# Inverses in two diagonal blocks with small products, an end in halves, squares added on DVE

## The chip, the cores and the metric

The kernel runs on one core of a Trainium2 chip. The metric is the device time of one execution in microseconds (us). PE is TensorE, DVE VectorE, ACT ScalarE, POOL GpSimd; SP issues most of the DMAs.

## The reference

One decoder block for 512 tokens of width 2048, in fp32. Two branches work on the normed input: RWKV-7 time mixing (16 heads of 64, a recurrence over the tokens) and a chunked spatial gate. They are mixed by sigmoid gates and added to the input; a SwiGLU layer of 5,632 hidden columns follows, and a last RMSNorm. Cut to what matters here:

```python
p = _rmsnorm(x, g) @ w_in                    # r, k, v, low-rank inputs, SGU input, gates
def step(S, inp):                            # RWKV-7, per head, S is 64 x 64
    sa = jnp.einsum('bhij,bhj->bhi', S, a_t)
    S = S * w_t[:, :, None, :] + sa[..., None] * b_t[:, :, None, :] + v_t[..., None] * k_t[:, :, None, :]
    y_t = jnp.einsum('bhij,bhj->bhi', S, r_t)
h = x + gates * branches
h = h + (silu(n(h) @ w_gate) * (n(h) @ w_up)) @ w_down
out = _rmsnorm(h, norm_final_g)
```

## The kernel before

Activations lie transposed, channels on partitions, 512 tokens along a row. Each fp32 product is made of three fp32r matmuls: ACT casts a weight tile to `w_hi` (`hi_of`, L105), DVE subtracts to get `w_lo` (`lo_of`, L108), and `mm3` (L125 to L127) multiplies hi by hi, hi by lo and lo by hi. A scheduler that simulates the engines decides the order of instructions on each engine; `tc.high_priority()` moves work forward in it.

The work in order of time: *the start* (0 to about 50 us), where the input arrives, is scaled and split (`a`, L161) and its squares are summed (L213, L214); 12 blocks of r, k and v; from 416 us 16 *gate blocks* of 96 matmuls of 128x512 (`ps_big`), whose results (`gt`, L524) go to DRAM; the spatial gate, the merge, the SwiGLU layer, and the down-projection from 2280 us on.

The recurrence is done in 8 chunks of 64 tokens. For every head and chunk (128 units) a unit triangular 64x64 matrix, loaded as `Ld`, one unit per partition, is inverted by substitution on DVE: 63 steps of one multiply (L406) and one reduce (L408) for each of two halves of the rows, into `X`. `X` goes to DRAM (`d_x`), and the chain of 8 chunk steps loads each step's part as `cTI` (L428) and the operands as `crec` (L418). The chain's fp32 matmuls (L472, L481, L490, L508, L511) stand between block matmuls.

The down-projection has 44 tiles of hidden rows (k). Its *main loop* runs over two halves of the output (q = 0, 1) and 40 of the tiles. *The end* takes the other four tiles, for 256 tokens at a time (H0, then H1): `down_sq` loads and splits weights of two output tiles, multiplies, adds to `hA` (L733), squares on ACT and sums on POOL (L856); then come the sum over partitions by a ones matmul (L171), a reciprocal of two columns, a diagonal matrix `dg` and a matmul that spreads it (L179), and `scale_out` (L887 and L889), which stores pairs of tiles.

Of the kernel before, what the change touches and what calls it, by code (L numbers as in the profile page):

```python
# [9 lines left out]
F32 = mybir.dt.float32  # L10
# [41 lines left out]
def body(ctx: ExitStack, tc: tile.TileContext, xT, par, cst, w_l0, w_in, lup, gup, sguw, sgub, lng, lnb,  # L52
# [22 lines left out]
    d_x = dram.tile([2, 64, 64, 64], F32, name="d_x")  # L75
# [121 lines left out]
    for n in START:  # L197
        pl = None
        for k in range(k0, k0 + n):
            nc.sync.dma_start(out=xt[:, k, :], in_=xT[k])  # L200
            if pl is None:
                pl = chunk(w_l0, k0, n, 2 * LORA)
            nT.append(scaled_split(xt[:, k, :], P("g1", k), ap, "a"))
        pg = chunk(w_in[0], k0, n, 256)
        if k0 <= 4 < k0 + n:
            nc.sync.dma_start(out=cst_t, in_=cst)
            nc.sync.dma_start(out=ident, in_=cst[:, 0:128])
        for k in range(k0, k0 + n):
            if k == 0:
                act.activation(out=acc, in_=xt[:, 0, :], func=AF.Square)  # L210
                continue
            sq = st.tile([128, 512], F32, name="sq", bufs=3)
            act.activation(out=sq, in_=xt[:, k, :], func=AF.Square)  # L213
            pool.tensor_tensor(out=acc, in0=acc, in1=sq, op=ALU.add)  # L214
        k0 += n
        if k0 == KT:
            rms(acc, 4, rs_c, st.tile([128, 512], F32, name="sq", bufs=3), rs)
        block_mm(lo_ps, pl, KT, nT, (LORA, LORA))
        block_mm(g_ps, pg, KT, nT, (128, 128))
# [171 lines left out]
    with ExitStack() as cs:  # L391
        gtp = cs.enter_context(tc.tile_pool(name="gtp", bufs=1, side="right"))
        with tc.tile_pool(name="sub", bufs=1, side="right") as sb:
            Ld = sb.tile([128, 64, 64], F32, name="Ld")
            nc.sync.dma_start(out=Ld.rearrange("u s t -> u (s t)"), in_=d_l.rearrange("h u s t -> (h u) (s t)"))
            X = sb.tile([128, 64, 64], F32, name="X")
            pool.memset(X, 0.0)
            pool.memset(X.rearrange("u s t -> u (s t)")[:, 0:4096:65], 1.0)
            for t in range(1, 64):
                for s0, s1 in ((0, min(t, 32)), (32, t)):  # L400
                    n, k = s1 - s0, t - s0
                    if n <= 0:
                        continue
                    tmp = sb.tile([128, 2048], F32, name="tmp", bufs=1)
                    tv_ = tmp[:, 0:n * k].rearrange("u (s k) -> u s k", k=k)
# [10 lines left out]
        def load(c, hf):  # L416
            rec = cp.tile([128, 2304], F32, name="crec", bufs=4)
            nc.sync.dma_start(out=rec, in_=d_c[hf, c])  # L418
            ZY = rec[:, 0:1024].rearrange("r (f h t) -> r f h t", f=4, h=2)
            SLV = rec[:, 1024:2048].rearrange("r (f h t) -> r f h t", f=4, h=2)  # L420
            RB = rec[:, 2048:2304].rearrange("r (f t) -> r f t", f=4)
            SV = cp.tile([128, 4, 2, 64], F32, name="cSV", bufs=4)
            for h in range(2):
                ot = slice(64 - 64 * h, 128 - 64 * h)
                pool.tensor_copy(out=SV[ot, :, h, :], in_=SLV[ot, :, h, 64:128])
            TI = cp.tile([128, 4, 64], F32, name="cTI", bufs=4)
            for h in range(2):
# [417 lines left out]
    at2 = [x for k in range(MAIN // 2, NHID // 2) for x in hidden(k, fin, "z")]  # L845
    acc = fin.tile([128, 512], F32, name="acc3")
    H0, H1 = T1, T2
    rbs = rs[:, 0:256]

    def sum_sq(j, sl):  # L850
        if j == 0:
            act.activation(out=acc[:, sl], in_=hT[j][:, sl], func=AF.Square)
        else:
            sq = fin.tile([128, 512], F32, name="sq2", bufs=2)
            act.activation(out=sq[:, sl], in_=hT[j][:, sl], func=AF.Square)
            pool.tensor_tensor(out=acc[:, sl], in0=acc[:, sl], in1=sq[:, sl], op=ALU.add)  # L856

    def down_sq(b, ts):
        n = NHID - MAIN
        with tc.high_priority():  # L860
            wh, wl = down_w(w_dn[b // 4, MAIN:NHID, :, 256 * (b % 4):256 * (b % 4) + 256].rearrange("k r c -> r k c"),
                            n, 256)
        res = []
        for i in range(2):
            j = 2 * b + i
            ps = bank()[:, 0:256]
            for k in range(n):
                c = slice(128 * i, 128 * i + 128)
                mm3(ps, wh[:, k, c], wl[:, k, c], at2[k][0][:, ts], at2[k][1][:, ts], k == 0, k == n - 1)
            add(hT[j][:, ts], ps, hT[j][:, ts])  # L870
        for j in (2 * b, 2 * b + 1):
            if b == 7:
                sq = fin.tile([128, 512], F32, name="sq2", bufs=2)
                with tc.high_priority():
                    act.activation(out=sq[:, ts], in_=hT[j][:, ts], func=AF.Square)
                res.append(sq[:, ts])
# [4 lines left out]
    def scale_out(p, ts, rb, on_pool):

        for k in (2 * p, 2 * p + 1):
            o = hT[k][:, ts]
            if on_pool(k):
                act.mul(o, o, P("g3", k))
                pool.tensor_tensor(out=o, in0=o, in1=rbs, op=ALU.mult)  # L887
            else:
                dve.scalar_tensor_tensor(out=o, in0=o, scalar=P("g3", k), in1=rb, op0=ALU.mult, op1=ALU.mult)  # L889
        ks = slice(2 * p, 2 * p + 2)  # L890
        nc.sync.dma_start(out=out[ks, :, ts].rearrange("k p t -> p k t"), in_=hA[:, ks, ts])

    for b in range(8):
        sqs = down_sq(b, H0)
    col = cols.pop()
    dg = fin.tile([128, 512], F32, name="dg", bufs=2)
    rb = rms([acc[:, H0]] + sqs, 2, col, dg)
    act.copy(out=rbs, in_=rb)
    for b in range(8):
        sqs = down_sq(b, H1)  # L900
        scale_out(b, H0, rbs, lambda k: k % 2 == 1)
    col = cols.pop()
    dg = fin.tile([128, 512], F32, name="dg", bufs=2)
    rb = rms([acc[:, H1]] + sqs, 2, col, dg)
    act.copy(out=rbs, in_=rb)
    for p in range(8):
        scale_out(p, H1, rb, lambda k: k // 2 in (1, 4, 6))
# [81 lines left out]
```

## Time and profile before

| | us |
|---|---|
| median of three runs | 2787.81 (2785.8 to 2789.99) |
| the profiled execution, own time | 2787.32 |
| its span | 2785.6 |
| PE busy in it | 2717.0 |
| DVE busy | 1839.5 |
| ACT busy | 1009.0 |
| POOL busy | 123.6 |

The span runs from the first instruction to the last; 1.7 us of the profiled execution lie outside of it. PE is nearly always at work, so an average over the span tells little: what counts are the short stretches in which PE waits or runs at a lower granted clock.

### The profile page before, as it was taken

How to read it: one execution, taken by the hardware profiler on the slowest of the kernel's cores; microseconds unless marked ns; L12 is line 12 of the kernel's file. 1: busy time of each engine (PE TensorE's matmuls, PEld its weight loads, DVE VectorE, ACT ScalarE, POOL GpSimd, SP SyncE). 2: the span in 40 equal slices, each digit the busy share in tenths (PEclk: the TensorE clock that was granted, in tenths of full speed). 3: DMA queues.
4: the chain of work that ended last, by engine and by line, in shares of the span. 5: the costliest groups of instructions: out<-in, count | busy, mean ns of one | idle time of the engine just before them, and what ended most of it. 6: DMA issues, size and time to landing. Idle time of an engine off the chain costs nothing.

```text
span 2785.6 us, 41408 instructions
## 1 busy us (share of the span) xinstructions
PE 2717.0 (98%) x17128; PEld 2410.0 (87%) x17128; DVE 1839.5 (66%) x2120; ACT 1009.0 (36%) x1239; POOL 123.6 (4%) x149
## 2 busy tenths in 40 slices
PE   8999999989999999999999999999999999999997
PEld 6888888777799878878799999999999998888887
DVE  6566668999554664435588888888888863333336
ACT  5445432211243332223344444443444432222224
POOL 3000000000111200000000000000000000000005
PEclk9999999999999999999999999999999999999998
DMA  5456664333764524434433433333433354444443
GB/s 169 116 149 154 172 162 151 106 108 105 244 206 145 185 96 140 141 114 148 148 118 118 122 114 122 113 121 113 123 115 118 121 186 159 144 147 148 139 156 122
DMA packets 200046, 388.46 MB, mean 139 GB/s; under 512 B 55857, under 2 KB 101041, under 8 KB 197553
## 3 DMA queue, kind: packets, MB, share of 16 engines
q1 hardware_dynamic: 199712, 385.74, 44.9%
q8 instruction: 134, 2.20, 0.3%
q14 instruction: 56, 0.45, 0.0%
q10 hardware_dynamic: 144, 0.07, 0.0%
HBM read 330.18 MB, written 55.57 MB: 138 GB/s over the span
## 4 chain that ended last, share of the span: by engine, by line
PE 84%; DVE 9%; issue 4%; DMA 1%; POOL 1%; ACT 0%; SPq 0%; POOLq 0%; DVEq 0%; ACTq 0%
PE ps_big L127 10%; PE ps_big L125 10%; PE ps_big L126 10%; PE rkps L125 6%; PE rkps L126 6%; PE rkps L127 6%; PE gB L725 4%; PE gB L727 4%; PE gB L726 4%; PE gA L725 3%; PE gA L727 3%; PE gA L726 3%; DVE tmp L406 3%; DVE w_lo L108 2%; DVE X L408 2%
## 5 line engine op out<-in xcount | busy, mean ns | idle before, releaser
L127 PE MATMUL ps_big<-a,w_lo 128*128 128x512 f32 (+1 forms) x1344 | 532.1, 396 | 28.4 <-DVE w_lo L108 28.4
L125 PE MATMUL ps_big<-a,w_hi 128*128 128x512 f32 (+1 forms) x1344 | 529.5, 394 | 9.0 <-ACT w_hi L105 9.0
L108 DVE TENSOR_TENSOR w_lo<-wq,w_hi 128x1024 fp32r<-128x1024 f32 x272 | 332.5, 1223 | 302.8 <-ACT w_hi L105 300.3
L126 PE MATMUL ps_big<-a,w_hi 128*128 128x512 f32 (+1 forms) x1344 | 528.7, 394 | 0.1
L105 ACT CAST w_hi<-wq 128x1024 fp32r<-128x1024 f32 x272 | 285.7, 1051 | 597.6 <-PE rkps L126 305.2
L108 DVE TENSOR_TENSOR w_lo<-w_raw,w_hi 128x1024 fp32r<-128x1024 f32 (+2 forms) x220 | 272.9, 1242 | 238.1 <-ACT w_hi L105 237.2
L105 ACT CAST w_hi<-w_raw 128x1024 fp32r<-128x1024 f32 (+2 forms) x220 | 225.6, 1030 | 502.2 <-PE ps_big L126 444.6
L127 PEld LDWEIGHTS ps_big<-a,w_lo 128*128 128x128 f32 (+1 forms) x1344 | 253.9, 189 | 94.9 <-DVE w_lo L108 40.4
L125 PEld LDWEIGHTS ps_big<-a,w_hi 128*128 128x128 f32 (+1 forms) x1344 | 254.0, 189 | 63.3 <-ACT w_hi L105 9.7
L126 PEld LDWEIGHTS ps_big<-a,w_hi 128*128 128x128 f32 (+1 forms) x1344 | 254.1, 189 | 55.4 <-DVE a L161 0.6
L125 PE MATMUL rkps<-xh,w_hi 128*128 128x512 f32 x640 | 248.8, 391 | 2.0 <-ACT xh L105 2.0
L126 PE MATMUL rkps<-xl,w_hi 128*128 128x512 f32 x640 | 249.5, 390 | 0.0
L127 PE MATMUL rkps<-xh,w_lo 128*128 128x512 f32 x640 | 249.4, 390 | 0.0
L725 PE MATMUL gB<-xsh,w_hi 128*128 128x256 f32 x704 | 200.2, 284 | 2.4 <-DVE u L733 2.0
L105 ACT CAST w_hi<-wt 128x1024 fp32r<-128x1024 f32 x132 | 138.4, 1049 | 175.6 <-PE gB L726 68.0
L726 PE MATMUL gB<-xsl,w_hi 128*128 128x256 f32 x704 | 200.0, 284 | 0.0
L727 PE MATMUL gB<-xsh,w_lo 128*128 128x256 f32 x704 | 199.9, 284 | 0.0
L108 DVE TENSOR_TENSOR w_lo<-wt,w_hi 128x1024 fp32r<-128x1024 f32 x132 | 161.4, 1223 | 32.6 <-ACT w_hi L105 32.6
L406 DVE TENSOR_TENSOR tmp<-X,Ld 128x1 f32<-128x1 f32 (+46 forms) x94 | 141.5, 1505 | 6.6 <-DMA Ld<-d_l 4.4
L125 PEld LDWEIGHTS rkps<-xh,w_hi 128*128 128x128 f32 x640 | 120.4, 188 | 27.4 <-ACT xh L105 2.2
L126 PEld LDWEIGHTS rkps<-xl,w_hi 128*128 128x128 f32 x640 | 120.5, 188 | 25.1
L127 PEld LDWEIGHTS rkps<-xh,w_lo 128*128 128x128 f32 x640 | 120.4, 188 | 25.0
(598 smaller groups left out, 5722.1 us busy)
## 6 DMA issues: line engine op xcount, KB each, us to landing
wq<-w_gu SPq DMA_DIRECT2D x176, 512.0 KB, 3.6
w_raw<-w_in SPq DMA_DIRECT2D x145, 512.0 KB, 4.0
wq<-w_dn SPq DMA_DIRECT2D x96, 512.0 KB, 4.1
wq<-d_hid SPq DMA_DIRECT2D x42, 512.0 KB, 3.6
crec<-d_c SPq DMA_DIRECT2D x16, 1152.0 KB, 7.4
w_raw<-w_out SPq DMA_DIRECT2D x32, 512.0 KB, 3.9
d_hid<-sl SPq DMA_DIRECT2D x44, 256.0 KB, 2.0
w_raw<-w_ps SPq DMA_DIRECT2D x16, 512.0 KB, 4.2
```

The costliest lines, as they stand in the source:

```text
L105: act.copy(out=dst, in_=src)
L108: (eng or dve).tensor_tensor(out=dst, in0=src, in1=hi.bitcast(F32), op=ALU.subtract)
L125: pe.matmul(out, wh, xh, start=start, stop=False)
L126: pe.matmul(out, wh, xl, start=False, stop=False)
L127: pe.matmul(out, wl, xh, start=False, stop=stop)
L406: dve.tensor_tensor(out=tv_, in0=X[:, s0:s1, s0:t], in1=Ld[:, s0:t, t].unsqueeze(1).to_broadcast([128, n, k]), op=ALU.mult)
L408: dve.tensor_reduce(out=X[:, s0:s1, t], in_=tv_, axis=AX.X, op=ALU.add)
L725: pe.matmul(bank, wh, xh, start=first and k == 0, stop=False, skip_group_check=True)
L726: pe.matmul(bank, wh, xl, start=False, stop=False, skip_group_check=True)
L727: pe.matmul(bank, wl, xh, start=False, stop=k == 7, skip_group_check=True)
```

## The change

It has three parts. *Start*: the 15 additions of squares go from POOL to DVE. *Inverses*: the substitution is done in the two 32x32 diagonal blocks alone, both in one instruction, 31 steps; two ACT copies turn the blocks of `Ld` into `LD`, so that each multiply reads a row. The off-diagonal block is the product of the first inverse, a block of `Ld` (`NB`) and the second inverse, made by PE as 2x128 matmuls of 32x32 in four groups of 32 partitions, with the inverses stored to DRAM (`d_dt`, `d_dx`) and loaded in another layout (`R1`, `R2`). The result (`XO`) is stored too (`d_xo`), and each `cTI` is put together from three loads in place of one, and a zeroed quarter. *End*: the weights of the last four tiles are loaded and split once, in the second half of the main loop, and kept (`wzp`); squares are added on DVE; the norm sums with 256-column ones matmuls and takes a reciprocal of 256 columns; the first 256 tokens (TA) are scaled on DVE alone; the last stores are of four tiles each.

```diff
@@ start
-            pool.tensor_tensor(out=acc, in0=acc, in1=sq, op=ALU.add)
+            dve.tensor_tensor(out=acc, in0=acc, in1=sq, op=ALU.add)
@@ substitution
-            for t in range(1, 64):
-                for s0, s1 in ((0, min(t, 32)), (32, t)):
...
-                    dve.tensor_tensor(out=tv_, in0=X[:, s0:s1, s0:t],
-                                      in1=Ld[:, s0:t, t].unsqueeze(1).to_broadcast([128, n, k]), op=ALU.mult)
-                    dve.tensor_reduce(out=X[:, s0:s1, t], in_=tv_, axis=AX.X, op=ALU.add)
-            nc.sync.dma_start(out=d_x.rearrange("h u s t -> (h u) (s t)"), in_=X.rearrange("u s t -> u (s t)"))
+            four = lambda t: t.rearrange("h (G g) s t -> g s (h G) t", g=4)
+            for g in range(4):
+                q = slice(32 * g, 32 * g + 32)
+                nc.sync.dma_start(out=NB[q], in_=four(d_l)[g, 0:32, :, 32:64])
...
+            for b in range(2):
+                q = slice(32 * b, 32 * b + 32)
+                act.copy(out=LD[:, b], in_=Ld[:, q, q].rearrange("u s t -> u t s"))
...
+            for t in range(1, 32):
+                tmp = sb.tile([128, 2048], F32, name="tmp", bufs=1)
+                tv_ = tmp[:, 0:2 * t * t].rearrange("u (b s k) -> u b s k", b=2, k=t)
+                dve.tensor_tensor(out=tv_, in0=D_[:, :, 0:t, 0:t],
+                                  in1=LD[:, :, t, 0:t].unsqueeze(2).to_broadcast([128, 2, t, t]), op=ALU.mult)
+                dve.tensor_reduce(out=D_[:, :, 0:t, t], in_=tv_, axis=AX.X, op=ALU.add)
+            DT = sb.tile([128, 32, 32], F32, name="R2")
+            act.copy(out=DT, in_=D_[:, 0].rearrange("u s t -> u t s"))
+            nc.sync.dma_start(out=d_dt.rearrange("h u s t -> (h u) (s t)"), in_=DT.rearrange("u s t -> u (s t)"))
+            nc.sync.dma_start(out=d_dx.rearrange("h u b s t -> (h u) (b s t)"), in_=D_.rearrange("u b s t -> u (b s t)"))
...
+            for r, src in ((R1, d_dt), (R2, d_dx[:, :, 1])):
+                for g in range(4):
+                    nc.sync.dma_start(out=r[32 * g:32 * g + 32], in_=four(src)[g])
+            XO = sb.tile([128, 32, 32], F32, name="XO")
+            for dst, w_, r in ((EB, NB, R1), (XO, EB, R2)):
+                for q in range(2):
+                    ps = rk.tile([128, 16, 32], F32, name="rkps", tag="rkps")
+                    for G in range(16):
+                        for g in range(4):
+                            p = slice(32 * g, 32 * g + 32)
+                            pe.matmul(ps[p, G, :], w_[p, 16 * q + G, :], r[p, 16 * q + G, :], start=True, stop=True,
+                                      tile_position=(32 * g, 32 * g))
+                    act.copy(out=dst[:, 16 * q:16 * q + 16], in_=ps)
+            nc.sync.dma_start(out=d_xo, in_=XO)
@@ load of a chain step
-                nc.sync.dma_start(out=TI[64 * h:64 * h + 64],
-                                  in_=d_x[h, 32 * hf + c:32 * hf + 32:8].rearrange("f s t -> s f t"))
+                lo_, up_ = slice(64 * h, 64 * h + 32), slice(64 * h + 32, 64 * h + 64)
+                pool.memset(TI[up_, :, 0:32], 0.0)
+                for b, p in ((0, lo_), (1, up_)):
+                    nc.sync.dma_start(out=TI[p, :, 32 * b:32 * b + 32],
+                                      in_=d_dx[h, 32 * hf + c:32 * hf + 32:8, b].rearrange("f s t -> s f t"))
+                g0 = 16 * h + 8 * hf + c // 4
+                nc.sync.dma_start(out=TI[lo_, :, 32:64],
+                                  in_=d_xo[32 * (c % 4):32 * (c % 4) + 32, g0:g0 + 7:2, :])
@@ down-projection and end
+            if q == 1 and k % 4 == 3 and k < 32:
+                wz.append(down_w(w_dn[k // 16, MAIN:NHID, :, 256 * (k // 4 % 4):256 * (k // 4 % 4) + 256].rearrange(
+                    "k r c -> r k c"), NHID - MAIN, 256, wzp))
+            if q == 1 and k in (33, 35):
+                at2 += hidden(MAIN // 2 + (k - 33) // 2, fin, "z")
...
+    def token_norm(parts, ts):
+
+        ps, rb = bank()[:, 0:256], bank()[:, 0:256]
+        for q, t in enumerate(parts):
+            pe.matmul(ps, ones, t, start=q == 0, stop=q == len(parts) - 1)
+        with tc.high_priority():
+            act.activation(out=rs[:, ts], in_=ps, func=AF.Sqrt, scale=1.0 / D, bias=eps[:, 0:1])
+            dve.reciprocal(out=rb, in_=rs[:, ts])
+            act.copy(out=rs[:, ts], in_=rb)
+        return rb
...
+    for j in range(KT):
+        sqs = [down_rest(j, TA)] if j < 15 else sqs + [down_rest(j, TA)]
+    for j in range(KT):
+        sqs_b = [down_rest(j, TB)] if j < 15 else sqs_b + [down_rest(j, TB)]
+        if j == 1:
+            token_norm([acc[:, TA]] + sqs, TA)
+        if j >= 4 and j % 2 == 1:
+            scale_out(j - 5, 2, TA, rs[:, TA], ())
+    scale_out(12, 4, TA, rs[:, TA], ())
+    rb = token_norm([acc[:, TB]] + sqs_b, TB)
+    for q in range(4):
+        scale_out(4 * q, 4, TB, rb, (2, 3, 7, 10, 11, 14))
```

The scheduler's order at three places follows. DVE at the start, before: the scalings `a` and the subtracts `w_lo`, up to the subtract of 3x192 columns for which PE waits.

```order
L161 SCALAR_TENSOR_TENSOR a<-xt,par_t,a 128x512 x3
L108 TENSOR_TENSOR w_lo<-w_raw,w_hi 128x512
L108 TENSOR_TENSOR w_lo<-w_raw,w_hi 128x3x192
L161 SCALAR_TENSOR_TENSOR a<-xt,par_t,a 128x512
L108 TENSOR_TENSOR w_lo<-w_raw,w_hi 128x768
L161 SCALAR_TENSOR_TENSOR a<-xt,par_t,a 128x512 x6
L108 TENSOR_TENSOR w_lo<-w_raw,w_hi 128x3x192
```

DVE at the same place now, where the additions (L216) stand between the scalings (L163).

```order
L163 SCALAR_TENSOR_TENSOR a<-xt,par_t,a 128x512
L216 TENSOR_TENSOR acc<-acc,sq 128x512 x2
L163 SCALAR_TENSOR_TENSOR a<-xt,par_t,a 128x512
L216 TENSOR_TENSOR acc<-acc,sq 128x512
L163 SCALAR_TENSOR_TENSOR a<-xt,par_t,a 128x512
L216 TENSOR_TENSOR acc<-acc,sq 128x512
L110 TENSOR_TENSOR w_lo<-w_raw,w_hi 128x512
L110 TENSOR_TENSOR w_lo<-w_raw,w_hi 128x3x192
L163 SCALAR_TENSOR_TENSOR a<-xt,par_t,a 128x512
L110 TENSOR_TENSOR w_lo<-w_raw,w_hi 128x768
```

Six pairs of a scaling and an addition follow, and then the second subtract of 3x192; up to it there are 11 scalings, 10 additions and four subtracts (before: 10 scalings, four subtracts).

PE in the gate blocks before, at the place of the chain's first matmuls (L472), in the fifteenth of the 16 blocks.

```order
L125 MATMUL ps_big<-a,w_hi 128x512
L472 MATMUL rkps<-cSV,crec 64x64
L126 MATMUL ps_big<-a,w_hi 128x512
L127 MATMUL ps_big<-a,w_lo 128x512
L472 MATMUL rkps<-cSV,crec 64x64 x7
```

PE now, in the seventh block, 821 block matmuls ahead of that place: the products of `NB` and `R1` and of `EB` and `R2` (L434).

```order
L128 MATMUL ps_big<-a,w_hi 128x512
L434 MATMUL rkps<-R_3279,NB 32x32 x6
L129 MATMUL ps_big<-a,w_lo 128x512
...
L129 MATMUL ps_big<-a,w_lo 128x512
L434 MATMUL rkps<-R_3279,NB 32x32 x122
L434 MATMUL rkps<-R_3280,EB 32x32 x128
L127 MATMUL ps_big<-a,w_hi 128x512
```

22 block matmuls stand between the first six products and the others, and 47 between the last product and the first matmul of the chain, in the eighth block. `Ld` lands 394 block matmuls ahead of the first product.

DVE at the end now: the additions of tokens TB (L767), the reciprocal of TA's norm (L924) and the scalings of TA (L914).

```order
L767 TENSOR_TENSOR acc_23824<-acc_23824,up 128x256
L924 RECIPROCAL rkps<-rs 128x256
L767 TENSOR_TENSOR hA<-rkps,hA 128x256
L914 SCALAR_TENSOR_TENSOR hA<-hA,par_t,rs 128x256 x6
L767 TENSOR_TENSOR acc_23824<-acc_23824,sl 128x256
L914 SCALAR_TENSOR_TENSOR hA<-hA,par_t,rs 128x256 x2
L767 TENSOR_TENSOR hA<-rkps,hA 128x256
L914 SCALAR_TENSOR_TENSOR hA<-hA,par_t,rs 128x256 x7
L767 TENSOR_TENSOR hA<-rkps,hA 128x256
```

Before, eight scalings of H0 stood there in one piece, and behind them subtracts `w_lo` and additions in turn.

## Rows read from the trace of the kernel before

**Rows 1.** The page: busy time, share of the span and instructions of each engine.

```profile
PE 2717.0 (98%) x17128; PEld 2410.0 (87%) x17128; DVE 1839.5 (66%) x2120; ACT 1009.0 (36%) x1239; POOL 123.6 (4%) x149
```

**Rows 2.** Windows of PE: length, busy (instructions), granted clock, DMA share, GB/s.

```profile
426.80:733.90 307.10, 286.24 (x1215) 0.99 0.38 119
733.90:760.40 26.50, 23.09 (x218) 0.87 0.93 319
2300.00:2700.00 400.00, 400.00 (x1766) 1.00 0.46 148
2718.20:2741.40 23.20, 23.20 (x193) 1.00 0.52 164
2718.20:2771.10 52.90, 50.03 (x399) 0.97 0.35 112
```

**Rows 3.** Timeline of PE at the start: start, length, instruction, [idle before, releaser].

```profile
16.32 0.50 PE L127 MATMUL ps_big<-a,w_lo 128*128 128x512 f32 x1 [2.08 <-DVE w_lo L108]
...
32.55 0.74 PE L127 MATMUL ps_big<-a,w_lo 128*96 128x512 f32 x1 [5.42 <-DVE w_lo L108]
...
36.46 0.40 PE L127 MATMUL ps_big<-a,w_lo 128*96 128x512 f32 x1
```

**Rows 4.** Timelines of DVE and of POOL at the start.

```profile
9.40 5.19 DVE L161 SCALAR_TENSOR_TENSOR a<-xt,par_t,a 128x512 fp32r<-128x512 f32 x3
...
30.69 1.81 DVE L108 TENSOR_TENSOR w_lo<-w_raw,w_hi 128x576 fp32r<-128x576 f32 x1
...
36.30 1.40 DVE L161 SCALAR_TENSOR_TENSOR a<-xt,par_t,a 128x512 fp32r<-128x512 f32 x2
...
16.61 17.02 POOL L214 TENSOR_TENSOR acc<-acc,sq 128x512 f32<-128x512 f32 x10 [0.89 <-ACT sq L213]
```

**Rows 5.** Groups of DVE, 426 to 735 us, last four by form; PE's waits.

```profile
L406 DVE TENSOR_TENSOR tmp<-X,Ld 128x1 f32<-128x1 f32 (+46 forms) x94 | 141.5, 1505 | 6.6 <-DMA Ld<-d_l 4.4
L408 DVE TENSOR_REDUCE X<-tmp 128x1 f32<-128x1 f32 (+46 forms) x94 | 86.8, 923 | 2.3
L108 DVE TENSOR_TENSOR w_lo<-w_raw,w_hi 128x1024 fp32r<-128x1024 f32 x51 | 62.0, 1218 | 0.5 <-ACT w_hi L105 0.5
...
L406 DVE TENSOR_TENSOR tmp<-X,Ld 128x2016 f32<-128x2016 f32 x1 | 3.9, 3850 | 0.0
L406 DVE TENSOR_TENSOR tmp<-X,Ld 128x961 f32<-128x961 f32 x2 | 3.8, 1914 | 0.0
...
L408 DVE TENSOR_REDUCE X<-tmp 128x31 f32<-128x961 f32 x2 | 2.3, 1156 | 0.1
...
L408 DVE TENSOR_REDUCE X<-tmp 128x32 f32<-128x2016 f32 x1 | 2.3, 2254 | 0.0
...
PE ps_big L127 <- DVE w_lo L108: 20.9, 21, 2.2
```

**Rows 6.** Timeline of PE: matmuls of the chain (x counts passes).

```profile
738.89 1.12 PE L472 MATMUL rkps<-cSV,crec 128*64 128x64 f32 x14
...
760.42 1.15 PE L472 MATMUL rkps<-cSV,crec 128*64 128x64 f32 x32
...
765.59 1.15 PE L481 MATMUL rkps<-cZ,cTI 64*64 64x64 f32 x32
```

**Rows 7.** DMA: count, KB, us to landing; and SP's timeline.

```profile
crec<-d_c SPq DMA_DIRECT2D x16, 1152.0 KB, 7.4
...
cTI<-d_x SPq DMA_DIRECT2D x32, 64.0 KB, 4.5
...
797.59 2.56 SPq L428 DMA_DIRECT2D cTI<-d_x  x4
```

**Rows 8.** Groups of DVE by form, whole span.

```profile
L889 DVE SCALAR_TENSOR_TENSOR hA<-hA,par_t,rs 128x256 f32<-128x256 f32 x8 | 7.2, 968 | 1.2 <-ACT rs L898 1.2
...
L889 DVE SCALAR_TENSOR_TENSOR hA<-hA,par_t,rkps 128x256 f32<-128x256 f32 x10 | 4.0, 476 | 1.7 <-ACT rs L905 1.7
...
L741 DVE RECIPROCAL rs<-rs 128x512 f32<-128x512 f32 x1 | 3.3, 3345 | 0.0
```

More of the change, by code (lines that the diff above doesn't have):

```diff
@@ L74, in body @@
     d_l = dram.tile([2, 64, 64, 64], F32, name="d_l")
-    d_x = dram.tile([2, 64, 64, 64], F32, name="d_x")
+    d_dx = dram.tile([2, 64, 2, 32, 32], F32, name="d_dx")
+    d_dt = dram.tile([2, 64, 32, 32], F32, name="d_dt")
+    d_xo = dram.tile([128, 32, 32], F32, name="d_xo")
     d_y = dram.tile([8, 128, 512], F32, name="d_y")
@@ L393, in body @@
         with tc.tile_pool(name="sub", bufs=1, side="right") as sb:
+            NB = sb.tile([128, 32, 32], F32, name="NB")
+            EB = sb.tile([128, 32, 32], F32, name="EB")
             Ld = sb.tile([128, 64, 64], F32, name="Ld")
             nc.sync.dma_start(out=Ld.rearrange("u s t -> u (s t)"), in_=d_l.rearrange("h u s t -> (h u) (s t)"))
-            X = sb.tile([128, 64, 64], F32, name="X")
-            pool.memset(X, 0.0)
-            pool.memset(X.rearrange("u s t -> u (s t)")[:, 0:4096:65], 1.0)
@@ L399, in body @@
-            for t in range(1, 64):
-                for s0, s1 in ((0, min(t, 32)), (32, t)):
[L401 to L405, printed above, removed]
-                    dve.tensor_tensor(out=tv_, in0=X[:, s0:s1, s0:t],
-                                      in1=Ld[:, s0:t, t].unsqueeze(1).to_broadcast([128, n, k]), op=ALU.mult)
-                    dve.tensor_reduce(out=X[:, s0:s1, t], in_=tv_, axis=AX.X, op=ALU.add)
@@ L409, in body @@
-            nc.sync.dma_start(out=d_x.rearrange("h u s t -> (h u) (s t)"), in_=X.rearrange("u s t -> u (s t)"))
+            four = lambda t: t.rearrange("h (G g) s t -> g s (h G) t", g=4)
+            for g in range(4):
+                q = slice(32 * g, 32 * g + 32)
+                nc.sync.dma_start(out=NB[q], in_=four(d_l)[g, 0:32, :, 32:64])
+            LD = sb.tile([128, 2, 32, 32], F32, name="LD")
+            D_ = sb.tile([128, 2, 32, 32], F32, name="D_")
+            pool.memset(D_, 0.0)
@@ new lines, in body @@
+            for b in range(2):
+                q = slice(32 * b, 32 * b + 32)
+                act.copy(out=LD[:, b], in_=Ld[:, q, q].rearrange("u s t -> u t s"))
+                pool.memset(D_[:, b].rearrange("u s t -> u (s t)")[:, 0:1024:33], 1.0)
+            for t in range(1, 32):
[4 more added lines that the diff above has]
+                dve.tensor_reduce(out=D_[:, :, 0:t, t], in_=tv_, axis=AX.X, op=ALU.add)
@@ new lines, in body @@
+            DT = sb.tile([128, 32, 32], F32, name="R2")
+            act.copy(out=DT, in_=D_[:, 0].rearrange("u s t -> u t s"))
+            nc.sync.dma_start(out=d_dt.rearrange("h u s t -> (h u) (s t)"), in_=DT.rearrange("u s t -> u (s t)"))
+            nc.sync.dma_start(out=d_dx.rearrange("h u b s t -> (h u) (b s t)"), in_=D_.rearrange("u b s t -> u (b s t)"))
+            R1 = sb.tile([128, 32, 32], F32, name="R1")
+            R2 = sb.tile([128, 32, 32], F32, name="R2")
+            for r, src in ((R1, d_dt), (R2, d_dx[:, :, 1])):
+                for g in range(4):
+                    nc.sync.dma_start(out=r[32 * g:32 * g + 32], in_=four(src)[g])
@@ L801, in body @@
     hA = ctx.enter_context(tc.tile_pool(name="hAp", bufs=1, reuse_waits="tile")).tile([128, KT, 512], F32, name="hA")
+    wzp = ctx.enter_context(tc.tile_pool(name="wzp", bufs=8, reuse_waits="tile"))
     hT = [hA[:, j, :] for j in range(KT)]
+    wz, at2 = [], []
     def bank(name="dk"):
@@ L815, in hidden, with down_w @@
         return [(hi[:, q, :], lo[:, q, :]) for q in range(2)]
-    def down_w(src, n, w):
-        p = (wp, gr)[wn[0] % 2]
-        wn[0] += 1
+    def down_w(src, n, w, p=None):
+        if p is None:
+            p = (wp, gr)[wn[0] % 2]
+            wn[0] += 1
         raw = raw_tile().rearrange("p (n w) -> p n w", w=w)
         nc.sync.dma_start(out=raw, in_=src)
-        hi = p.tile([128, n, w], F32R, name="w_hi", tag="w_hi", bufs=2, padded_shape=[128, 1024 // w, w])
-        lo = p.tile([128, n, w], F32R, name="w_lo", tag="w_lo", bufs=2, padded_shape=[128, 1024 // w, w])
+        hi = p.tile([128, n, w], F32R, name="w_hi", tag="w_hi", bufs=8 if p is wzp else 2, padded_shape=[128, 1024 // w, w])
+        lo = p.tile([128, n, w], F32R, name="w_lo", tag="w_lo", bufs=8 if p is wzp else 2, padded_shape=[128, 1024 // w, w])
         hi_of(hi, raw)
@@ L844, in body @@
                 add(hT[8 * q + i], outs[i], hT[8 * q + i])
-    at2 = [x for k in range(MAIN // 2, NHID // 2) for x in hidden(k, fin, "z")]
     acc = fin.tile([128, 512], F32, name="acc3")
[L847 to L856, printed above, removed]
@@ L858, in down_sq @@
-    def down_sq(b, ts):
-        n = NHID - MAIN
-        with tc.high_priority():
[L861 to L869, printed above, removed]
-            add(hT[j][:, ts], ps, hT[j][:, ts])
[L871 to L876, printed above, removed]
-            else:
-                sum_sq(j, ts)
-        return res
@@ L881, in scale_out @@
[L881 to L907, printed above, removed]
+    TA, TB = T1, T2
@@ new lines, in down_rest @@
+    def down_rest(j, ts):
+        n = NHID - MAIN
+        ps = bank()[:, 0:ts.stop - ts.start]
+        wh, wl = wz[j // 2]
+        c = slice(128 * (j % 2), 128 * (j % 2) + 128)
+        for k in range(n):
+            mm3(ps, wh[:, k, c], wl[:, k, c], at2[k][0][:, ts], at2[k][1][:, ts], k == 0, k == n - 1)
+        sq = gp_.tile([128, 512], F32, name=("sl", "up")[j % 2], bufs=2)[:, ts]
+        with tc.high_priority():
+            add(hT[j][:, ts], ps, hT[j][:, ts])
+            act.activation(out=acc[:, ts] if j == 0 else sq, in_=hT[j][:, ts], func=AF.Square)
+            if 0 < j < 14:
+                add(acc[:, ts], acc[:, ts], sq)
+        return sq
@@ new lines, in scale_out @@
+    def scale_out(k, n, ts, rb, on_pool):
+        for i in range(k, k + n):
+            o = hT[i][:, ts]
+            if i in on_pool:
+                act.mul(o, o, P("g3", i))
+                pool.tensor_tensor(out=o, in0=o, in1=rs[:, ts], op=ALU.mult)
+            else:
+                dve.scalar_tensor_tensor(out=o, in0=o, scalar=P("g3", i), in1=rb, op0=ALU.mult, op1=ALU.mult)
+        nc.sync.dma_start(out=out[k:k + n, :, ts].rearrange("k p t -> p k t"), in_=hA[:, k:k + n, ts])
+    def token_norm(parts, ts):
[7 more added lines that the diff above has]
+        return rb
```

## The prediction

> **What bounds the kernel now.** I read the page first, then the stretches of TensorE (PE), then what PE waits for in the bad stretches. PE is busy for 98% of the span [rows 1], so an edit shortens the run only if it takes PE work away or a PE wait. In the down-projection, where PE never stops, 1,766 matmuls of 512 columns take 400.0 us, 0.2265 us each [rows 2]. Against that price three stretches lose time, and they are the three that are edited.
>
> - *Start.* PE stands still until 32.55 us, 5.42 us of it for one `w_lo` subtract of DVE, and its next nine matmuls, up to 36.46, are 0.43 us apart: half the clock [rows 3]. DVE is late because each of its instructions costs more than double while POOL adds squares: three `a` scalings take 5.19 us (1.73 each) at 9.40, two take 1.40 (0.70 each) at 36.30, after POOL's additions (16.61 to 33.63) have ended [rows 4].
> - *Middle.* From the landing of `Ld` at 426.8 to the place where PE comes to the chain at 733.9, 1,215 block matmuls take 307.1 us; at 0.2265 they take 275.2. So 31.9 us are lost [rows 2], 20.9 of them in 21 waits for `w_lo` [rows 5]: a subtract of 1.2 us stands behind multiplies and reduces of up to 3.85 and 2.25 us, 228.3 us of substitution in all [rows 5]. In the next 26.5 us PE does 57 block matmuls (12.9 us) and 160 short ones (4.8 us at 0.03, the price below) and loses 8.8 at a clock of 0.87 [rows 2]. Together 40.7.
> - *End.* From 2718.2 to 2771.1 PE does 32 outputs of 12 matmuls of 256 columns. In the undisturbed part 193 take 23.2 us, 0.12 each [rows 2], so 46.1 of 52.9 us is work and 6.8 is norm and low clock. 14.5 us follow to the end of the span.
>
> **Start: −7.2 us.** The 15 additions go from POOL to DVE. A 512-element pass costs 0.70 uncontended [rows 4]; an addition, by the line through the two reduces of [rows 5] (2.254 and 1.156 us for 2,016 and 961 elements: 1.04 ns per element plus 0.155), 0.69. By the order DVE does 11 scalings, 10 additions and four subtracts (2,432 elements, 3.1 us) up to the second 3x192 subtract; without POOL that is 11×0.70 + 10×0.69 + 3.1 = 17.7 us from 9.4, so 27.1, in place of 30.69 + 1.81 = 32.5. PE resumes 5.4 earlier. With the shorter wait I also take back the low clock, 9×(0.43−0.23) = 1.8, together 7.2. Bounds: −2 if ACT's squares or the input loads set the pace instead, −9.3 if the 2.08 us wait for a `w_lo` at 16.32 [rows 3] goes as well.
>
> **Middle: −14.7 us.** DVE's work falls from 69,472 to 20,832 elements per pass, in 31 steps. Each reduce keeps its price: 31×0.155 + 20,832×0.00104 = 26.5 us. The multiply is open: with `Ld` read at a stride it costs 3.850 and 1.914 us for 2,016 and 961 elements, 1.835 ns each [rows 5]; the new one reads a transposed copy in order, and the `w_lo` row (1.218 us for 1,024, read in order) lies on the reduces' line. I take that line: 26.5 as well, 53 in all; at the strided price 43 and 69.5. Between the first and the last step DVE's order holds 14 `w_lo` and 6 `gt`, some 20 us, so 73.
>
> PE comes to the first product 394 block matmuls after `Ld` lands: 89.2 us at 0.2265. The data: two ACT copies (2.1 us, priced as 1,024-element passes), 73 for DVE, one more copy (1), then a store and loads of 128 KB, which I put at two trips of 6 us, between the 4.5 of a 64 KB `cTI` and the 7.4 of a `crec` [rows 7]: 88. A tie; `w_lo` waits delay both sides.
>
> What the middle will lose then: 256 products. FP32 makes two passes of each (16 matmuls of the chain are 32 records), so 512 passes. The nearest row: 32 passes of 128x64 weights in 1.15 us, so 0.030 each after the first; 64x64 ones the same [rows 6]. 15.4 us, with a gap at each end 16; bounds 8 (half) and 35 (the 14 at low clock: 1.12 us, 0.069 each [rows 6]). Waits for `w_lo` during 89 us: 3 (0 to 14; before, 0.4 us per `w_lo`, but behind pieces half as long). Between products, `EB` must be copied by ACT: 2. Chain start: `XO` is stored, reloaded into `cTI`, behind `crec` on SP: 5 (1 to 9). Sum 26 in place of 40.7. All bounds at once on one side give −30, on the other +19, which none of the cases below comes to. Three more table loads on ACT and the zeroing on POOL lie beside PE's blocks.
>
> Of TensorE's overhead the Trainium skill ("TensorEngine Tiling (Array Packing)", Instruction Overhead) says that a matmul has about 60 cycles on TRN2 that a small free size does not undercut; an estimate by it, 512 passes of 25 ns, is 12.8 us, and the sum would come 3 us lower than by the row.
>
> **End: −4.6 us.** Sixteen loads and splits of weights (1.22 us DVE each) become eight inside the second main loop. Their cover is that loop, where PE never waits [rows 2]; uncovered they cost 8×1.22 = 10. PE then has 46.1 us plus six passes of the ones matmul, 1.0: 47.1, −5.8. Behind TA's norm DVE has a burst of 16 scalings with only three PSUM additions between. The same form took 0.968 us beside scalings on POOL and 0.476 where its second operand lay in PSUM [rows 8]. POOL now rests there, as DVE's 0.70 and 1.73 at the start also tell the two apart, so I take 0.476: 9 us of burst with its additions, while PE makes 6 outputs into 8 banks: no wait. At 0.968 the burst is 17.5 us and PE waits some 4.5. After the last matmul: a reciprocal of 256 (half of 3.345 [rows 8], 1.7) replaces a tiny one, `dg` and the second broadcast: +0.5; the first store waits for four tiles: +0.7. So −5.8+1.2 = −4.6; bounds 0 and −7.
>
> **Sum.** The profiled execution took 2787.3, 0.5 below the median. 2787.3 − 7.2 − 14.7 − 4.6 = 2760.8; with the 0.5, 2761.
>
> **Rivals.**
> - *The multiply keeps its strided price.* Its output and `D_` still lie in short rows, which speaks for it; that `w_lo` and the reduces share one line speaks against. DVE then needs 16.5 us more, PE stands before the first product for some 15: 2776.
> - *The products run at half clock.* The wait of 5.42 us was followed by half clock [rows 3], and the stretch from 733.9 has a mean of 0.87 [rows 2]. If PE idles long ahead of the 250 products, 512×(0.069−0.030) = 20 more: 2781. Against it: the clock came back while 512-column matmuls ran, and 28 of these stand between the first six products and the rest.
> - *Four groups at the same time.* The groups lie on different rows and columns of the array. If four passes run in the time of one, 512 cost 4 us and not 16: 2749. The 64x64 passes of the chain, which also use two quadrants in turn, are no faster than the 128x64 ones [rows 6], which speaks against it. The Trainium skill ("TensorEngine Tiling (Array Packing)", Key Properties) says that different tiles run in parallel; no run yet shows 32x32 ones.
> - *Slower: SP's queue.* The loads of `cTI` go from 4 to 12 per chain step, at 0.64 us each on SP [rows 7], 5.1 us more per step, and weight loads stand behind them. If all of it reaches PE, 8×5.1 = 41: 2802. It decides from 26.5/8 = 3.3 us per step on. Against it: 8 steps share 9 gate blocks of 21.7 us, and the loads are issued a step ahead into four buffers.
>
> **How the numbers follow.** Chances: forecast 0.57 (2752 to 2771), strided multiply 0.15, half clock 0.08, four at a time 0.13, SP 0.07. The predicted time is the likeliest, 2761. The range 2745 to 2780 takes in the first, second and fourth and half of the third; some 1.2 in 10 is left out. Within 0.2% (5.6 us, about what a measurement of this kernel can tell) lie half of the half-clock case and a little of the strided one, 0.06; slower is SP, 0.07; the rest, 0.87, is faster.
>
> **What would show it.** Start: DVE's `a` at 0.70 from 9 us on and PE's wait at 27, not 32.5. Middle: DVE's multiply of 1,922 elements at 2.15 us (strided: 3.7); PE's first product at about 509 (426.8 + 89.2 − 7.2) with a wait under 3 us; 512 passes in 16 us; the first chain matmuls, 69 block matmuls and the sum of 26 us behind it, near 550 instead of 737. End: no `w_lo` after the main loop, PE without a gap of over 1 us up to TB's norm, some 14.5 us plus 1.2 after it. The prediction is wrong if PE waits at the products for more than about 10 us, or if blocks beside the chain, free of waits before, wait for `w_raw`.

## The result, and the profile after

The changed kernel takes 2751.55 us (median of four runs, 2749.01 to 2752.09) against 2787.43 (four runs of the kernel before, beside them); the ratio is 0.9867, interval 0.9852 to 0.9882. The forecast was 2761, the range 2745 to 2780. The stages below are those of the two profiled executions.

Start times of the same matmuls of PE cut the span into stages. One stage is compared with the same stage, so a gain made earlier does not blur it.

| stage, up to | before | after | difference |
|---|---|---|---|
| first low-rank matmul | 106.70 | 98.15 | −8.55 |
| first matmul of the merge | 916.91 | 894.78 | −22.13 |
| first matmul of the down-projection | 1257.68 | 1257.87 | +0.19 |
| first matmul of its last four tiles | 436.95 | 436.98 | 0.0 |
| last product of these | 52.55 | 47.23 | −5.32 |
| end of the span | 14.81 | 14.89 | +0.1 |
| span | 2785.6 | 2749.9 | −35.7 |

The forecast had −7.2, −14.7 and −4.6 for start, middle and end. Where the whole run gained 9 us more than that, the middle holds 7.4 of it.

The page of the changed kernel, where [rows 1] stood:

```profile
PE 2708.9 (99%) x17624; PEld 2408.6 (88%) x17624; DVE 1672.3 (61%) x2033; ACT 1012.5 (37%) x1233; POOL 73.7 (3%) x133
```

Its start, PE and DVE in order of time, where [rows 3, 4] stood:

```profile
14.61 0.50 PE L129 MATMUL ps_big<-a,w_lo 128*128 128x512 f32 x1 [0.41 <-DVE w_lo L110]
25.73 0.47 PE L129 MATMUL ps_big<-a,w_lo 128*96 128x512 f32 x1 [0.30 <-DVE w_lo L110]
```

```profile
9.27 0.75 DVE L163 SCALAR_TENSOR_TENSOR a<-xt,par_t,a 128x512 fp32r<-128x512 f32 x1
...
24.92 0.75 DVE L110 TENSOR_TENSOR w_lo<-w_raw,w_hi 128x576 fp32r<-128x576 f32 x1
```

A scaling `a` at 9 us costs 0.75 instead of 1.73, the second 3x192 subtract ends at 25.7 although DVE has done ten additions more since 9.27, and the waits of 2.08 and 5.42 us are 0.41 and 0.30.

Windows of PE in the middle and at the end, as in [rows 2], and PE's waits over the stage of the inverses:

```profile
418.25:507.36 89.11, 89.11 (x395) 1.00 0.53 163
507.36:539.81 32.45, 25.68 (x582) 0.79 0.68 180
539.81:753.00 213.19, 213.12 (x1962) 1.00 0.58 185
2687.78:2735.01 47.23, 47.23 (x390) 1.00 0.14 46
```

```profile
PE rkps L434 <- issue: 6.4, 3, 3.2
PE ps_big L573 <- DVE w_lo L110: 1.2, 1, 1.2
PE rkps L646 <- POOL vz L635: 0.8, 1, 0.8
PE rkps L434 <- DMA R<-d_dt: 0.3, 1, 0.3
```

No matmul waits for `w_lo` from the landing of `Ld` to the first product (before: 21 waits, 20.9 us [rows 5]). From there to the chain the whole loss lies in the 32.45 us around the products: 69 block matmuls account for 15.6, so 16.8 are lost. From the first chain matmul on, at 539.81 instead of 737.33, PE is full again up to 753; the two waits of 1.2 and 0.8 us in the list come behind that.

DVE's groups of the substitution, and its longest instructions, where [rows 5] stood:

```profile
L415 DVE TENSOR_TENSOR tmp<-D__3176,LD 128x2 f32<-128x2 f32 (+30 forms) x31 | 26.6, 857 | 2.7 <-ACT LD L410 2.0
L417 DVE TENSOR_REDUCE D__3176<-tmp 128x2 f32<-128x2 f32 (+30 forms) x31 | 26.4, 853 | 0.8
...
L415 DVE TENSOR_TENSOR tmp<-D__3176,LD 128x1922 f32<-128x1922 f32 x1 | 2.2, 2162 | 0.0
L417 DVE TENSOR_REDUCE D__3176<-tmp 128x62 f32<-128x1922 f32 x1 | 2.2, 2151 | 0.0
```

26.6 and 26.4 us: the two 26.5 of the forecast. PE's timeline at the products (x counts passes, two per product):

```profile
507.36 0.76 PE L434 MATMUL rkps<-R,NB 32*32 32x32 f32 x12
...
513.61 2.02 PE L434 MATMUL rkps<-R,NB 32*32 32x32 f32 x212 [0.28 <-DMA R<-d_dt]
518.82 0.65 PE L434 MATMUL rkps<-R,NB 32*32 32x32 f32 x32 [3.19 <-issue]
519.27 1.48 PE L434 MATMUL rkps<-R,EB 32*32 32x32 f32 x95
522.39 1.93 PE L434 MATMUL rkps<-R,EB 32*32 32x32 f32 x128 [1.64 <-issue]
525.85 0.65 PE L434 MATMUL rkps<-R,EB 32*32 32x32 f32 x33 [1.53 <-issue]
526.42 0.80 PE L127 MATMUL ps_big<-a,w_hi 128*128 128x512 f32 x1
...
531.71 0.42 PE L127 MATMUL ps_big<-a,w_hi 128*128 128x512 f32 x1
```

212 passes take 2.02 us, 8.5 ns apart (2.02 less 0.22 for the last, by 211): the rival of four groups at a time. Then PE stops three times for something that no engine and no transfer releases ("issue"), and between two stops it does 127 or 128 passes. From 513.61 to 526.42 it is 12.8 us, and twelve block matmuls behind take 5.29 us, 0.44 each: half clock, 2.6 us.

DVE at the end, where [rows 8] stood:

```profile
2716.65 1.76 DVE L924 RECIPROCAL rkps<-rs 128x256 f32<-128x256 f32 x1 [1.36 <-ACT rs L923]
...
2718.85 2.46 DVE L914 SCALAR_TENSOR_TENSOR hA<-hA,par_t,rs 128x256 f32<-128x256 f32 x6
```

0.41 per scaling, with POOL at rest, and PE goes through both halves without a gap.

### The profile page after: what moved, and what is told of

Read it like the earlier page. It is cut to its first block, busy times and chain, and to the rows that moved or that the text cites. A ratio compares the mean times of both kernels' runs of the same rounds, so it can differ in the third digit from the quotient of the medians.

```text
span 2749.9 us, 42330 instructions
## 1 busy us (share of the span) xinstructions
PE 2708.9 (99%) x17624; PEld 2408.6 (88%) x17624; DVE 1672.3 (61%) x2033; ACT 1012.5 (37%) x1233; POOL 73.7 (3%) x133
## 5 line engine op out<-in xcount | busy, mean ns | idle before, releaser
L110 DVE TENSOR_TENSOR w_lo<-wq,w_hi 128x1024 fp32r<-128x1024 f32 x264 | 322.2, 1223 | 275.9 <-ACT w_hi L107 273.3
L107 ACT CAST w_hi<-wq 128x1024 fp32r<-128x1024 f32 x264 | 276.8, 1051 | 562.0 <-PE rkps L128 236.7
L110 DVE TENSOR_TENSOR w_lo<-w_raw,w_hi 128x1024 fp32r<-128x1024 f32 (+2 forms) x220 | 266.7, 1214 | 348.0 <-ACT w_hi L107 336.6
L127 PEld LDWEIGHTS rkps<-xh,w_hi 128*128 128x128 f32 x640 | 120.3, 188 | 27.1 <-ACT xh L107 2.2
L759 PEld LDWEIGHTS gB<-xsh,w_hi 128*128 128x128 f32 x704 | 135.9, 193 | 3.5 <-issue 2.2
```

Of the source, the lines that this page charges most:

```text
L107: act.copy(out=dst, in_=src)
L110: (eng or dve).tensor_tensor(out=dst, in0=src, in1=hi.bitcast(F32), op=ALU.subtract)
L127: pe.matmul(out, wh, xh, start=start, stop=False)
L759: pe.matmul(bank, wh, xh, start=first and k == 0, stop=False, skip_group_check=True)
```

## The experiments

**Which part gave what.** Three kernels each take one part of the change back. The first puts the additions on POOL again:

```diff
-            dve.tensor_tensor(out=acc, in0=acc, in1=sq, op=ALU.add)
+            pool.tensor_tensor(out=acc, in0=acc, in1=sq, op=ALU.add)
```

> The changed kernel with the 15 additions of squares back on POOL, nothing else. Theory (each part's gain stays where it was made): the stage up to the first low-rank matmuls takes the 8.55 us longer that the two traces differ there, 2751.6 + 8.5 = 2760, and PE again stands over 5 us for a w_lo near 32 us. Rival (the later stages would have taken the gain back, or the end and the middle hide it): 2752 to 2755.

It took 2760.43 us (ratio to the kernel before 0.9899, 0.9885 to 0.9912). The stage up to the low-rank matmuls is 107.68 long, the others are within 1.2 us of the changed kernel's. PE's timeline has the old wait and the old half clock behind it:

```profile
33.79 0.74 PE L129 MATMUL ps_big<-a,w_lo 128*96 128x512 f32 x1 [4.92 <-DVE w_lo L110]
34.33 0.63 PE L127 MATMUL ps_big<-a,w_hi 128*96 128x512 f32 x1
```

The second has the main loop and the end as before:

```diff
-            if q == 1 and k % 4 == 3 and k < 32:
-                wz.append(down_w(...))
+    for b in range(8):
+        sqs = down_sq(b, H0)
...
```

> The changed kernel with the down-projection and the end as before, nothing else. Theory: PE's stretch over the last four tiles grows from 47.2 to 52.6 us and what follows the last product stays at 14.9, so +5.3: 2757. Rival (the splits moved into the main loop cost something there, which undoing gives back): under 2755, with the main loop shorter than the 436.8 us it takes now.

2755.56 us (0.9883, 0.987 to 0.9897), 4.0 above the changed kernel. The stretch of the last four tiles is 52.57 (+5.34), the main loop 436.96, as long as with the eight splits in it (436.98): they cost nothing there. In this execution the middle took 893.19, 1.59 less than in the changed kernel, and what follows the last product 14.04, 0.85 less. So stages that the edit leaves alone also differ by over 1 us between two executions, and 1.3 missing in the total are no more than that.

The third has the substitution over 64 columns and `d_x` again:

```diff
-            for t in range(1, 32):
+            for t in range(1, 64):
+                for s0, s1 in ((0, min(t, 32)), (32, t)):
...
```

> The changed kernel with the substitution over 64 columns in two halves, one load per inverse and no products, as before; the start and the end stay changed. Theory: 22.1 us come back, 2774, and the chain's first matmul is back at about 728. Rival (start and inverse are not independent: a substitution that starts 8.5 us earlier in the run meets other loads): off by more than 3 us from 2774.

2773.6 us (0.9947, 0.9934 to 0.9961), 22.0 above the changed kernel; first chain matmul at 728.50, and 22 waits for `w_lo` of 21.9 us in sum are back. By the medians 8.9, 4.0 and 22.0 add to 34.9 of the 35.9 gained: the parts are independent but for about 1 us, as much as the medians of the kernel before differ, beside the changed kernel and beside these three (2787.43 and 2788.64).

**Does POOL slow DVE?** Fifteen additions run on POOL on a tile that nothing waits for:

```diff
             dve.tensor_tensor(out=acc, in0=acc, in1=sq, op=ALU.add)
+            pool.tensor_tensor(out=idle, in0=idle, in1=idle, op=ALU.add)
```

> The changed kernel with 15 additions of the same size on POOL beside the 15 on DVE, on a tile of their own that nothing waits for. Theory (DVE slows while POOL works on SBUF): DVE's scalings a take 1.5 to 1.8 us while POOL runs, PE waits for w_lo at the start again, +5 to +9, 2757 to 2761. Rival (POOL's additions were slow and late, and DVE was not hindered by them): DVE's rows stay at 0.70, 2752.

2761.32 us, and the stage up to the low-rank matmuls took 108.47 (+10.3). The times of this kernel and of the next three are of one execution each, so their stages count for more than their totals. Timelines of POOL and DVE:

```profile
1.41 19.58 POOL L219 TENSOR_TENSOR idle<-idle 128x512 f32<-128x512 f32 x15
```

```profile
20.02 1.52 DVE L163 SCALAR_TENSOR_TENSOR a<-xt,par_t,a 128x512 fp32r<-128x512 f32 x1
21.46 0.68 DVE L218 TENSOR_TENSOR acc<-acc,sq 128x512 f32<-128x512 f32 x1
22.07 1.35 DVE L110 TENSOR_TENSOR w_lo<-w_raw,w_hi 128x512 fp32r<-128x512 f32 x2
23.34 0.74 DVE L163 SCALAR_TENSOR_TENSOR a<-xt,par_t,a 128x512 fp32r<-128x512 f32 x1
```

POOL stops at 20.99, and DVE's instructions halve from the next one on (1.52 to 0.74 for the same scaling). Nothing depends on POOL here, so the time is DVE's own being hindered; by what path POOL hinders it was not tried. The size came out a little over the 5 to 9 expected.

**What set the multiply's price?** The copies into `LD` are left unturned, so that the second operand is read at a stride again:

```diff
-                act.copy(out=LD[:, b], in_=Ld[:, q, q].rearrange("u s t -> u t s"))
+                act.copy(out=LD[:, b], in_=Ld[:, q, q])
...
-                                  in1=LD[:, :, t, 0:t].unsqueeze(2).to_broadcast([128, 2, t, t]), op=ALU.mult)
+                                  in1=LD[:, :, 0:t, t].unsqueeze(2).to_broadcast([128, 2, t, t]), op=ALU.mult)
```

> The changed kernel with the two ACT copies into LD left unturned, so that the multiply reads its second operand at a stride, as before; the same numbers are computed. Theory (the stride of that operand set the old price of 1.835 ns per element): the multiply of 1,922 elements takes 3.7 us in place of 2.16, DVE is 16 us later, PE stands some 15 us ahead of the products: 2767. Rival (the price came from the shape, or from X): 2.2 us, no wait, 2752.

2767.23 us, 15.7 above the changed kernel, and the groups by form read:

```profile
L415 DVE TENSOR_TENSOR tmp<-D__3176,LD 128x1922 f32<-128x1922 f32 x1 | 3.7, 3718 | 0.0
L417 DVE TENSOR_REDUCE D__3176<-tmp 128x62 f32<-128x1922 f32 x1 | 2.2, 2153 | 0.0
```

The stride alone makes the difference between 2.16 and 3.72 us. PE's waits add up to 5.4 us for `R1` and 4.9 for `w_lo`, and the chain starts at 555.20, 15.4 later than in the changed kernel.

**Do four groups work at the same time?** All products run in the first group of 32 partitions; the other three groups of the off-diagonal blocks are zero:

```diff
-                            p = slice(32 * g, 32 * g + 32)
+                            p = slice(0, 32)
...
-                                      tile_position=(32 * g, 32 * g))
-                    act.copy(out=dst[:, 16 * q:16 * q + 16], in_=ps)
+                                      tile_position=(0, 0))
+                    act.copy(out=dst[0:32, 16 * q:16 * q + 16], in_=ps[0:32])
```

> The changed kernel with all products in the first group of 32 partitions, one after the other; the other three groups of the off-diagonal blocks are zero, so the output lacks them. As many matmuls and records as now. Theory (four groups work at the same time, which makes a pass 8.5 ns): in one group a pass takes 30 ns, 512 take 15.4 us without pauses, in place of 13.2 with them: 2753. Rival (a 32x32 pass is short by itself): 8.5 ns and the pauses as now, 2752.

2759.51 us, more than either theory gave. Timeline of PE, and windows (busy, passes that touch the window, clock):

```profile
507.59 10.80 PE L436 MATMUL rkps<-R,NB 32*32 32x32 f32 x256
518.21 13.84 PE L436 MATMUL rkps<-R,EB 32*32 32x32 f32 x256
531.98 0.80 PE L129 MATMUL ps_big<-a,w_lo 128*128 128x512 f32 x1
```

```profile
509.50:511.50 2.00, 2.00 (x69) 1.00 1.11 109
511.50:513.50 2.00, 2.00 (x51) 0.64 0.94 136
513.50:515.50 2.00, 2.00 (x42) 0.50 0.66 99
```

At full clock 69 passes touch a window of 2.00 us. The first of them began up to a pass's length, 0.22 us, ahead of it, so they start 32 ns apart ((2.00 + 0.22) / 69), near the 30 of the chain in [rows 6]; that price stands for one group, 8.5 for four. There is no "issue" pause. The surplus is the clock: at 0.50 the second 256 passes take 13.77 us (518.21 to 531.98), 54 ns each, where 32 ns would make 8.2. Key Properties of "TensorEngine Tiling (Array Packing)" in the Trainium skill has different tiles work in parallel; the trace agrees, with 8.5 against 32 ns.

**What are the three pauses?** Two kernels. One does each product twice, which doubles the passes and their code but no copy and no load:

```diff
-                            pe.matmul(ps[p, G, :], w_[p, 16 * q + G, :], r[p, 16 * q + G, :], start=True, stop=True,
-                                      tile_position=(32 * g, 32 * g))
+                            for again in range(2):
+                                pe.matmul(ps[p, G, :], w_[p, 16 * q + G, :], r[p, 16 * q + G, :], start=True, stop=True,
+                                          tile_position=(32 * g, 32 * g))
```

> The changed kernel with every product done twice in a row, the second over the first. 512 passes more. Theory A (code loading sets the pace, 3.5 us per packet of 128 passes): four more packets, +14 us, 2766, with a pause after each 128 passes. Rival (a pass costs 8.5 ns and the three pauses have other causes): +4.4, 2756, with three pauses as now.

2765.27 us. PE's timeline, the transfers of the same stretch by queue, and PE's waits:

```profile
506.82 0.47 PE L435 MATMUL rkps<-R,NB 32*32 32x32 f32 x24
...
512.21 2.14 PE L435 MATMUL rkps<-R,NB 32*32 32x32 f32 x201
518.98 2.16 PE L435 MATMUL rkps<-R,NB 32*32 32x32 f32 x128 [4.63 <-issue]
...
533.17 1.99 PE L435 MATMUL rkps<-R,EB 32*32 32x32 f32 x128 [1.47 <-issue]
536.62 1.98 PE L435 MATMUL rkps<-R,EB 32*32 32x32 f32 x128 [1.47 <-issue]
540.07 0.68 PE L435 MATMUL rkps<-R,EB 32*32 32x32 f32 x32 [1.47 <-issue]
```

```profile
q8 instruction: 7, 0.11, 1.5%
```

```profile
PE rkps L435 <- issue: 13.6, 7, 4.6
```

Seven pauses, and seven packets of 16 KB on the instruction queue (0.11 MB); between two pauses stand 127 or 128 passes, a weight load and a matmul each, 3.45 us from start to start (536.62 − 533.17). The packets also fall where the pauses are: in windows of 0.5 us they begin in those from 516.5, 520.0, 523.5, 527.0, 530.5, 534.0 and 537.5, so that each of the seven restarts (518.98 to 540.07) comes 2.4 to 2.7 us behind the start of such a window. In the changed kernel the three do so in those from 516.0, 520.0 and 523.0, ahead of 518.82, 522.39 and 525.85. The Trainium skill, "Runtime: NRT & Kernel Launch", Instruction fetch mechanics, has each engine's code refilled in blocks of 16 KiB, 256 instructions, and calls that mostly hidden. The block agrees with the trace; hidden it is not where 128 passes run in 1.1 us. From the first product to the first pause run 225 passes (24 + 201) and 21 block matmuls between them; in the changed kernel it is 224 (12 + 212) and 22, the same 246 in all: the code had been loaded up to the same place.

The other kernel gives the loading time to happen behind long matmuls. It emits the first eight gate blocks ahead of the chain, with the products in four bursts of 64 between pieces of 24 block matmuls:

```diff
+            bursts = {(6, 2): lambda: burst(EB, NB, R1, 0), (6, 3): lambda: burst(EB, NB, R1, 1),
+                      (7, 0): lambda: burst(XO, EB, R2, 0), (7, 1): lambda: burst(XO, EB, R2, 1)}
+            for b in range(8):
+                gate_block(b, bursts)
+            nc.sync.dma_start(out=d_xo, in_=XO)
```

> The changed kernel with its products in four bursts of 64, with 24 block matmuls between them, in place of 6 and then 250 in a row; the first eight gate blocks are written ahead of the chain for it. Theory A (the pauses of 3.2, 1.6 and 1.5 us are the loading of PE's code, one packet of 16 KB per 128 passes, which short passes outrun): the passes go at 8.5 ns without a pause, the low clock behind them goes too, and the products' stretch loses some 6 us in place of 16.4: 2741. Rival B (the pauses belong to the products themselves, to the copy of EB by ACT or to the bank that it frees): only the copy's wait is hidden, 2 to 3 us, 2748 to 2750. Rival C (each change between whole matmuls and tiles of 32 costs microseconds): no gain or a loss, 2752 or more.

2739.56 us (0.9825, 0.9812 to 0.9838): faster than both kernels, 12.0 us below the changed one by the medians and 10.0 by the spans of the two profiled executions (2739.9 against 2749.9). Timeline of PE, and a window over the bursts:

```profile
515.92 1.29 PE L448 MATMUL rkps<-R,NB 32*32 32x32 f32 x128
517.14 0.50 PE L127 MATMUL ps_big<-a,w_hi 128*128 128x512 f32 x1
```

```profile
515.92:540.00 24.08, 24.08 (x595) 1.00 0.37 119
```

A burst of 128 passes costs 1.4 us with both changes of tile (1.5 us from the start of the block matmul ahead at 515.61 to 517.14, less its 0.23, and 0.1 for the slower one behind), no pause, clock 1.00. Four cost 5.6 us; the stretch of the changed kernel cost 16.8. Of these 11.2 us the stage keeps 8.75 (886.03 against 894.78); 0.8 more come back as waits for `w_lo` and POOL at the blocks behind the chain, and the remaining 1.6 were not followed. In the kernel with one group 128 passes take 4.1 us at full clock, more than the 3.45 of the loading, and there is no pause either. Three kernels and the times of the packets so agree that the pauses are the loading of code.

## Why the prediction was right, and where it was not

*The time*: 2751.55 lies at the lower edge of the band given to the forecast, 2752 to 2771, and nearer to the 2749 of the rival "four groups at the same time"; the stated range held because it took in that rival.

*What bounds the kernel, and the three places*: right; 34.9 of the 35.9 us return when the three parts are taken back one by one.

*Start, −7.2, measured −8.55.* The reason held (busy POOL makes the same DVE scaling 1.52 instead of 0.74). The POOL row of [rows 4] begins only at 16.61; that POOL was at work beside the three slow scalings from 9.40 is in this row of the kernel before:

```profile
9.35 6.37 POOL L214 TENSOR_TENSOR acc<-acc,sq 128x512 f32<-128x512 f32 x4 [0.29 <-ACT sq L213]
```

The subtract was expected at 27.1 and ended at 25.7; the 2.08 us wait, put into the bound alone, fell to 0.41 as well.

*Substitution.* 53 us, as forecast; the choice for the reduces' line and against the strided price was right, and the rival with that price is what the strided kernel shows: 15.7 us above the changed kernel, where the rival stood 15 above the forecast. PE came to the first product at 507.36 (509 expected; the start had gained 1.35 more). The data were not level with it: SP issued the last of the four loads of `R1` only at 507.42, and the products went on at 513.61, 95.4 us after `Ld` had landed, where 88 was forecast.

```profile
501.69 3.95 SPq L426 DMA_DIRECT2D R<-d_dt  x3
...
507.42 0.57 SPq L426 DMA_DIRECT2D R<-d_dt  x1
```

What kept PE's wait at 0.28 us are the 22 block matmuls that the order puts behind the first six products; the prediction names them, as 28, for the clock alone. That the tie cost nothing is to that extent luck.

*Middle, −14.7, measured −22.1.* Here the term of the new losses was mis-sized, 26 us against 16.8. By the losses alone, 40.7 and 16.8, the middle should have gained 23.9; where the other 1.8 went was not followed. Of the 8.8 that the prediction found behind 733.9 "at a clock of 0.87", 3.4 were one wait of the chain for POOL in the kernel before, which it does not name:

```profile
PE rkps L472 <- POOL cSV L425: 3.4, 1, 3.4
```

The parts of the new losses:

| part | forecast | measured |
|---|---|---|
| products | 16 | 12.8 (513.61 to 526.42) and 0.8 for the first six |
| waits for `w_lo` ahead | 3 | 0 |
| between products and for `R1` | 2 | 0.3 beside the 12.8 |
| start of the chain | 5 | 0 |
| half clock behind the products | none | 2.6 |

The price of a pass was wrong twice over. The rival "four at a time" was true, given 0.13, and passes cost 8.5 ns; but the 4 us in place of 16 did not come, since code loading sets a pace of 3.45 us per 128 passes, 27 ns each, nearly the 30 that had been taken. So the 16 came near the 13.6 measured by luck: a price 3.5 times too high, and a limit that the prediction did not have. The evidence against the rival, that 64x64 passes of the chain are no faster than 128x64 ones, does not carry over to tiles of 32 in four groups. The chain's start cost nothing. 47 block matmuls stand between the last product and the first chain matmul, 13.4 us as they ran (526.42 to 539.81), and the first matmul that reads `cTI` (L515) comes at 544.93; `XO` was stored at 527.17 and first loaded again at 531.86. The forecast counted the transfers and overlooked that cover. The two terms that came out as nothing, 3 and 5, are 8 of the 9.2 us by which the 26 were too many.

*Half clock*: it fell during the first pause (granted clock 1.00 up to 518 us, 0.50 from 519) and not ahead of the products, and with passes paced by their code it cost 2.6 us behind them, not 20.

*End, −4.6, measured −5.2.* PE's stretch 47.2 (47.1 forecast); the +1.2 behind the last product was +0.1, though the reciprocal (1.76) came as priced and a scaling took 0.41 where 0.476 had been taken; which of the two estimates in the +1.2 was too high was not followed.

*Slower by SP's queue*: the 96 small loads are there, and PE has no wait for `w_raw` or `cTI`.

## What to carry to other kernels

When an engine is full, add up its gaps by stage against the price of an undisturbed row; that gave two of three terms here to 1.4 us. Before paying for a new wait, count what stands between the work and its consumer in the order of the waiting engine. Tiny matmuls that share the array in four groups are paid, many in a row, by the loading of their instructions and not by the pass: put them in bursts between long ones, and their code is loaded meanwhile.

## What the runs showed of the hardware that was not expected

Short matmuls outrun the loading of their code: 128 passes of 32x32 in four groups run in 1.1 us when loaded and in 3.45 us when not; some 225, with 21 or 22 long matmuls among them, ran before the first pause. And the clock fell without any wait: in the kernel with one group PE was busy all the time from 507.5 us, with passes of one 32x32 tile, and the granted clock went from 1.00 (2.4 GHz) to 0.64 in the window from 511.5 and to 0.50 (1.2 GHz) from 513.5; in the kernel with bursts, where passes in four groups stand 1.3 us at a time between block matmuls, it stayed at 1.00 from 515.92 to 540.00. Why it fell was not tried further.
